# Layer 0's context gate and up in scaled fp16 parts, with their weights scanned in the projection's weight ring

## Chip, cores and metric

The kernel runs on one core of one Trainium2 chip. The metric is the device time in microseconds (us) of one execution; the median of the runs counts, and lower is better. The engines are TensorE (PE, matmuls), VectorE (DVE), ScalarE (ACT), GpSimd (POOL) and SyncE (SP). SP, ACT and POOL each issue DMAs from a queue of their own; an engine runs its rows in the order in which they stand.

## The reference

Two layers of a diffusion backbone over 1024 latent tokens and 256 context tokens, width 1024, in float32. Layer 0 mixes the tokens (Fourier groups beside a Hyena convolution), layer 1 has a neighbourhood attention; each ends in a feed-forward layer:

```python
def mixer_ab(u, w_in, w_out, ...):
    p = u @ w_in
    y_f = fourier_mix(p[..., :FOURIER_CH])
    y_h = hyena_mix(p[..., FOURIER_CH:], ...)
    return jnp.concatenate([y_f, y_h], axis=-1) @ w_out

def swiglu(u, w_gate, w_up, w_down):
    return (jax.nn.silu(u @ w_gate) * (u @ w_up)) @ w_down
```

`w_in` has 16 blocks of 128 columns, `w_gate` and `w_up` have 22 each (D_FF is 2816). The change is in layer 0's `swiglu` for the 256 context tokens, and in what is done during `p = u @ w_in`.

## The kernel before

**Parts and pieces.** Activations lie with their channels on the 128 partitions, in 8 blocks of 128 channels (KB = 8), and in three pieces of columns: two of 512 latent tokens (0 and 1) and the 256 context tokens (2). Precision comes from two parts, high and low: a product takes three matmuls (high x high, high x low, low x high). Parts come in two sorts. `weights` (L372) loads a tile of 512 KB, casts it on ACT to fp32r (L352, the tile `wh`) and subtracts on DVE (L354, `wl`). `weights16` multiplies by a scale and makes two fp16 parts, on ACT (L1948) and DVE (L1949), in one tile `hl`; for this the largest sum of absolute values of the weights must be known beforehand.

**Rings.** The pool `pw` (L323) has four buffers with the tag "ws" (tiles as they are loaded), two of "wh" and two of "wl". A new tile of a tag waits until the tile that had its buffer has been read for the last time. Users of "ws" are the weights of the projection, the tiles of the condition's weights (`ada_w`), the matrices of the long convolution (`mat`, `cs`) and, from the feed-forward layer on, `weights16`. `ld` (L333) issues on SP, `lda` (L336) on ACT, `ldr` (L339) on POOL.

**Order of the work.** A scheduler orders the instructions of each engine from the program's order and its own model of times; `follow(ins)` (L288) asks it to put instructions behind another one. The program's order is that of `run` (L2785):

- `in_proj` (L1104) goes through the 16 blocks of `w_in`: the first two as a pair, then one by one (loop over i, the text's block i), 72 matmuls each (8 channel blocks x 3 products x 3 pieces). Between the channel blocks it steps through `fill`: generators of other work (long filters, context filters, the condition's groups) with a number of steps for each i. From block 4 on a block ends in `short_conv` (L1087; ACT L1097, then DVE): its result z is spilled by SP, three DMAs for each z.
- Then the rest of the fill is drained; `turned` (L1306) transposes inputs, and `unit` (L1345) makes the long convolution with matmuls (L348) against matrices that `cast` loads through POOL and that `cmat2` (L416) casts on ACT.
- The output projection follows (`out_proj`, L1749). After each of its pieces it calls `after1`, which norms that piece for the feed-forward layer.
- `ffn(0)` (L2141) begins with the context stage: for each of 22 blocks a tile of gate and one of up, 24 matmuls of 256 columns each, Silu (L2188) and product. On the way each weight tile's absolute values are summed on ACT (L381, Abs with an accumulated sum, its output thrown away). After the 22 blocks `scale_w` (L1941 and around) makes the scales from these sums, by a reduction over the partitions on POOL and a chain on DVE. The latent tokens' part of gate and up needs the scales: it runs in scaled fp16 parts (L2095).
- Then down (its context part is L2484), the attention, and the second layer's feed-forward part, whose weights are scanned by `scan` (L1877) during `ffn(0)`: loads on ACT's queue into two tiles of another pool, one Abs each.

Of the kernel before, what the change touches and what calls it, by code (L numbers as in the profile page):

```python
# [13 lines left out]
AF = mybir.ActivationFunctionType  # L14
ALU = mybir.AluOpType
AX = mybir.AxisListType.X
MUL, ADD, SUB, MAX, MIN = ALU.mult, ALU.add, ALU.subtract, ALU.max, ALU.min

P = 128
D = 1024  # L20
KB = D // P
LAT = 1024
CTX = 256
NFB = 22
# [234 lines left out]
class Builder:  # L259
# [1608 lines left out]
    def scan(self, tiles, mark):  # L1868
# [4 lines left out]
        for k in range(n + 2):  # L1873
# [5 lines left out]
                    self.lda(t, tiles[k][0])  # L1879
            yield  # L1880

    def scale_u_begin(self):

        nc = self.nc
        t = self.cw[:, 20:28]
        for c in (0, 1):
            for j in (0, 1):
                nc.vector.tensor_reduce(t[:, 2 * j + c:2 * j + c + 1], self.ada[(1, c)][:, j * 8:j * 8 + 8], axis=AX, op=MAX,
                                        apply_absolute_value=True)
        nc.gpsimd.partition_all_reduce(t[:, 4:8], t[:, 0:4], channels=P, reduce_op=bass.bass_isa.ReduceOp.max)  # L1890
        return t
# [33 lines left out]
        self.turn = not getattr(self, "turn", False)  # L1925
        return self.S2() if self.turn else x()

    def scale_w(self, key, groups):

        nc = self.nc  # L1930
        sums = self.wsc[key]
        n = sums.shape[1] // 2
        nc.gpsimd.partition_all_reduce(sums[:, n:], sums[:, :n], channels=P, reduce_op=bass.bass_isa.ReduceOp.max)
        for j, k in enumerate(groups):
            t = self.C(2)
            s, inv = t[:, 0:1], t[:, 1:2]
            w = n // len(groups)
            nc.vector.tensor_reduce(s, sums[:, n + j * w:n + j * w + w], axis=AX, op=MAX)
            nc.vector.tensor_scalar(s, s, 1e-30, 1.0 / 8192.0, op0=MAX, op1=MUL)
            nc.vector.tensor_tensor(inv, s, self.xinv, MUL)  # L1940
            nc.vector.reciprocal(s, s)  # L1941
            self.wsc[k] = s, inv

    def split_scaled(self, src, t, s):

# [195 lines left out]
    def ffn(self, l, u, h, hs, second, after, keep=None, begun={}):  # L2141
# [29 lines left out]
        if u is None:  # L2171
            mx = self.mx
        else:
            wsums = self.C(4 * NFB)
            self.mx = mx = wsums[:, :8 * n2 - 4]
        if l == 0:
            self.pad(self.pt, PAD_T)
        if u is not None:
            self.wsc["here"] = wsums
            for fb in range(NFB):  # L2180
                wide = 3 if fb < NFB - 2 else 2
                gh, gl = self.weights(a["gate"][l, fb], wide=wide, sums=wsums[:, fb:fb + 1])
                uh, ul = self.weights(a["up"][l, fb], wide=wide, sums=wsums[:, NFB + fb:NFB + fb + 1])
                lo = self.last_lo
                ga = self.lin(gh, gl, 0, range(KB), u, (2,))[2]
                ua = self.lin(uh, ul, 0, range(KB), u, (2,))[2]
                t = self.T()
                nc.scalar.activation(t[:, :256], ga[:, :256], AF.Silu)  # L2188
                nc.vector.tensor_tensor(t[:, :256], ua[:, :256], t[:, :256], MUL)
                self.ldr(hidc[fb // 2][:, fb % 2], t[:, :256])  # L2190
                if fb >= 2:
                    with self.follow(last):
                        next(second, None)
                last = lo
            self.scale_w("here", [(0, 0), (0, 1)])
            self.load_cond(act=False)
            todo = self.ada_stream([(l1, m, (0, 1) if l1 == 0 or m < 2 else (0,))
                                    for l1, m in [(0, 5)] + [(1, m) for m in range(6)]], 30)
# [586 lines left out]
    def run(self):  # L2785
# [10 lines left out]
        def drain(g):  # L2796
            for _ in g:
                pass
# [21 lines left out]
        def filters():  # L2820
            gens = [self.filter_raw("l", raws["l"], (o,)) for o in (0, 1)]
            next(gens[0])
            yield
            for o in (0, 1):
                tot = self.filter_sum("l", o, raws["l"][o])
                for k, _ in enumerate(gens[o]):
                    if k > 1 and k % 2 == 0:
                        next(tot)
                    yield
                for k, _ in enumerate(self.spectrum_l(o, raws["l"][o], tot)):  # L2830
                    if o == 0 and k == 5:
                        next(gens[1])
                    yield

        long = filters()
        ada = self.late_groups((2, 3), "ws")
        filt = (x for o in (0, 1) for g in (self.filter_raw("c", raws["c"], (o,)), self.spectrum_c(o, raws["c"][o]))
# [8 lines left out]
        def conv():  # L2846
# [5 lines left out]

        fc, cc = four(), conv()
        self.in_proj(u, ng, ((long, (1, 2, 4, 5, 5, 5, 5, 5, 6, 0)), (filt, (0,) * 9 + (3, 3, 3, 3, 2)),
                             (ada, (0,) * 5 + (1, 1, 2, 1, 2, 1, 2, 1, 2, 1, 2))), fc, cc)
        self.held = False
        for i in range(8):
            self.tap(f"u{i}", u.ap(0, i, 0))
# [46 lines left out]
        uf = Act()  # L2905
# [10 lines left out]
        def after1(pcs):  # L2916
            spill(h, hs0, pcs)
            if 2 in pcs:
                uf.t.update(self.new_act(pcs=(2,)).t)
                rs = self.rms(pcs)  # L2920
                for b in range(KB):
                    self.norm_block({b: h.ap(0, b, 2)}, b, 2, 0, 3, uf, rs[0])
                self.half.add(0)
                self.scale_x(0, 3)
                load_h((1,))
                rest.append(rs[1])
            else:
                drain(first)
                rest.append(self.rms((1,))[0])
# [257 lines left out]
```

## Time and profile before

| | us |
|---|---|
| median of 3 runs (lowest, highest) | 2808.63 (2808.47, 2810.5) |
| profiled execution | 2803.95 |
| its span in the trace | 2802.2 |
| PE busy | 2692.3 |
| DVE busy | 2128.0 |
| ACT busy | 1629.4 |
| POOL busy | 507.4 |

The granted clock of the profiled execution is 0.986 of full speed. In the lines of the trace, the first number is the start in us from the span's start, the second a duration; then come the engine, the line of the kernel, the operation, output <- input, partitions x elements and type, and xN for N such instructions in a row. In brackets stands the engine's idle time before, and what ended it. In the window rows each engine has its busy us and, in brackets, its instructions. In the group rows stand, after the bar, the total busy us and the mean ns of one, then the idle time before. Matmuls overlap, so the price of one is read from the distance between starts.

### The profile page before, as it was taken

How to read it: one execution, taken by the hardware profiler on the slowest of the kernel's cores; microseconds unless marked ns; L12 is line 12 of the kernel's file. 1: busy time of each engine (PE TensorE's matmuls, PEld its weight loads, DVE VectorE, ACT ScalarE, POOL GpSimd, SP SyncE). 2: the span in 40 equal slices, each digit the busy share in tenths (PEclk: the TensorE clock that was granted, in tenths of full speed). 3: DMA queues.
4: the chain of work that ended last, by engine and by line, in shares of the span. 5: the costliest groups of instructions: out<-in, count | busy, mean ns of one | idle time of the engine just before them, and what ended most of it. 6: DMA issues, size and time to landing. Idle time of an engine off the chain costs nothing. (4 is left out here: it accounts for less than half of the span.)

```text
span 2802.2 us, 44493 instructions
## 1 busy us (share of the span) xinstructions
PE 2692.3 (96%) x15570; PEld 1713.0 (61%) x15570; DVE 2128.0 (76%) x3870; ACT 1629.4 (58%) x3005; POOL 507.4 (18%) x805
## 2 busy tenths in 40 slices
PE   7999789999999999999999999999999999999998
PEld 3877577878899444444446646767677544444444
DVE  6678788768877889986898736878786877775774
ACT  4434224443488566666656736888774656664653
POOL 0210233351101111121011002333221012221000
PEclk9999899999999999999999999999999999999999
DMA  7345636766645787787987746788955246654863
GB/s 273 111 156 171 190 106 186 231 205 224 232 162 172 257 297 288 284 313 268 362 311 278 237 155 160 190 207 196 252 180 196 85 144 223 222 193 167 296 223 105
DMA packets 312318, 595.92 MB, mean 213 GB/s; under 512 B 83353, under 2 KB 130139, under 8 KB 312095
## 3 DMA queue, kind: packets, MB, share of 16 engines
q1 hardware_dynamic: 242238, 381.76, 42.7%
q0 software_dynamic: 51456, 149.99, 15.4%
q10 hardware_dynamic: 18400, 61.35, 6.2%
q8 instruction: 122, 2.00, 0.3%
q14 instruction: 102, 0.83, 0.1%
HBM read 445.64 MB, written 119.80 MB: 202 GB/s over the span
## 5 line engine op out<-in xcount | busy, mean ns | idle before, releaser
L2095 PE MATMUL ps<-s,s 128*128 128x512 f16 x2280 | 509.0, 379 | 6.3 <-DVE s L2119 3.6
L2095 PEld LDWEIGHTS <-s 128*128 128x128 f16 x2640 | 258.1, 98 | 321.2 <-issue 11.1
L348 PE MATMUL ps<-s,wh 128*128 128x256 f32 (+1 forms) x1784 | 409.8, 333 | 7.9 <-ACT wh L352 5.8
L348 PEld LDWEIGHTS ps<-s,wh 128*128 128x128 f32 x1784 | 298.9, 191 | 43.1 <-ACT wh L352 8.4
L2359 PE MATMUL ps<-s 128*128 128x512 f16 (+2 forms) x1404 | 316.1, 376 | 0.2 <-ACT s L2349 0.2
L2359 PEld LDWEIGHTS <-s 128*128 128x128 f16 x1716 | 166.2, 98 | 196.1 <-issue 5.3
L348 PE MATMUL ps<-s,wl 128*128 128x256 f32 (+1 forms) x892 | 272.6, 332 | 3.5 <-DVE wl L354 3.5
L2349 ACT ACTIVATE s<-s,c 128x512 f16<-128x512 f32 (+1 forms) x300 | 200.3, 715 | 116.9 <-DMA s<-d 63.0
L348 PE MATMUL ps<-s,s 128*128 128x65 f16 (+4 forms) x2748 | 241.6, 239 | 17.2 <-DVE s L2722 3.8
L2350 DVE SCALAR_TENSOR_TENSOR s<-s,c,s 128x512 f16<-128x512 f32 (+1 forms) x300 | 208.7, 749 | 30.6 <-ACT s L2349 30.3
L339 POOL DMA_DIRECT2D d<-s x245 | 132.9, 544 | 503.9 <-DVE s L2212 169.7
L2095 PE MATMUL ps<-s,hl 128*128 128x512 f16 x924 | 212.2, 379 | 1.7 <-ACT hl L1948 1.7
L348 PE MATMUL pq<-s,hl 128*128 128x512 f16 (+1 forms) x960 | 208.0, 360 | 0.4 <-DVE s L2602 0.4
L348 PEld LDWEIGHTS ps<-s,wl 128*128 128x128 f32 x892 | 167.6, 191 | 22.4 <-DVE wl L354 5.2
L2095 PEld LDWEIGHTS <-hl 128*128 128x128 f16 x1056 | 103.2, 98 | 126.4 <-ACT hl L1948 1.9
L1948 ACT ACTIVATE hl<-ws,c 128x1024 f16<-128x1024 f32 x89 | 101.8, 1144 | 109.6 <-DMA ws<-in_up 39.1
L1949 DVE SCALAR_TENSOR_TENSOR hl<-ws,c,hl 128x1024 f16<-128x1024 f32 x89 | 114.0, 1284 | 62.3 <-ACT hl L1948 62.1
L348 PEld LDWEIGHTS <-s 128*128 128x128 f16 x2400 | 115.1, 98 | 66.0 <-issue 4.6
L348 PEld LDWEIGHTS ps<-s,s 128*128 128x128 f32 (+1 forms) x828 | 128.8, 192 | 33.8 <-PE ps L348 8.9
L1949 DVE SCALAR_TENSOR_TENSOR s<-t,c,s 128x512 f16<-128x512 f32 x176 | 127.0, 750 | 26.4 <-ACT s L1948 26.4
L348 PEld LDWEIGHTS <-hl 128*128 128x128 f16 x960 | 87.0, 98 | 81.0 <-issue 10.0
L1948 ACT ACTIVATE s<-t,c 128x512 f16<-128x512 f32 x176 | 118.1, 714 | 9.2 <-DVE t L2074 5.6
(538 smaller groups left out, 5109.4 us busy)
## 6 DMA issues: line engine op xcount, KB each, us to landing
s<-d SPq DMA_DIRECT2D x326, 256.0 KB, 4.8
d<-s POOLq DMA_DIRECT2D x229, 256.0 KB, 4.4
s<-in_down SPq DMA_DIRECT2D x150, 256.0 KB, 5.9
ws<-in_gate SPq DMA_DIRECT2D x42, 512.0 KB, 4.7
ws<-in_up SPq DMA_DIRECT2D x42, 512.0 KB, 6.3
s<-in_ada_w POOLq DMA_DIRECT2D x34, 512.0 KB, 6.5
d<-s SPq DMA_DIRECT2D x60, 256.0 KB, 2.8
s<-in_ada_w ACTq DMA_DIRECT2D x30, 512.0 KB, 7.7
```

The costliest lines, as they stand in the source:

```text
L339: self.last_ldr = self.nc.gpsimd.dma_start(out, in_).ins
L348: self.last_mm = self.nc.tensor.matmul(o, l, r, start=st, stop=sp).ins
L1948: self.last_hi = self.nc.scalar.activation(hi, src, AF.Copy, scale=s).ins
L1949: self.last_lo = self.nc.vector.scalar_tensor_tensor(lo, src, s, hi, op0=MUL, op1=SUB).ins
L2095: nc.tensor.matmul(ps, x[:, sl], y, start=first and j == 0 and x is wh and y is xh, stop=j == 3 and x is wl, skip_group_check=True)
L2349: self.last_hi = nc.scalar.activation(x, f[:, c:c + 512], AF.Copy, scale=s).ins
L2350: self.last_lo = nc.vector.scalar_tensor_tensor(y, f[:, c:c + 512], s, self.raw_part(x), op0=MUL, op1=SUB).ins
L2359: m = nc.tensor.matmul(acc[j][:, c0:c1], x[:, sl], y[:, xs], start=first and k == 0, stop=last and k == 2, skip_group_check=True)
```

## The change

Two things are changed together.

First, the context stage takes its gate and up tiles through `weights16` in place of `weights`: two scaled fp16 parts in `hl`, from the ring "ws". The context's activations `uf` become fp16 parts too. The scales are thus needed before the stage: `after1` calls `scale_both` (scales for the activations of latent and context tokens together) and `scale_w`, which stood after the 22 blocks; `scale_x` goes. Silu takes the inverse scale of gate, and the product with up that of up. The number of matmuls stays.

Second, the sums of absolute values come from a pass of their own over the 44 tiles, `scan_ring`: it loads each tile on ACT's queue into the ring "ws" and sums it with an Abs on ACT, two loads ahead. It is one more generator of the fill of `in_proj`, with 6 steps in each of the positions 2 to 5 of the fill (24 steps, which run during the blocks 3 to 6); the rest is drained right after `in_proj`, and POOL's reduction over the partitions follows there.

```diff
+    def scan_ring(self, tiles, mark):
+        nc = self.nc
+        n = len(tiles)
+        st = []
+        for k in range(n + 2):
+            with self.follow(mark()):
+                if k > 1:
+                    t = st.pop(0)
+                    nc.scalar.activation(t, t, AF.Abs, accum_out=tiles[k - 2][1])
+                if k < n:
+                    st.append(self.W("ws", "ws"))
+                    self.lda(st[-1], tiles[k][0])
+            yield
...
+    def scale_both(self, m):
...
+        nc.gpsimd.partition_all_reduce(r, t, channels=P, reduce_op=bass.bass_isa.ReduceOp.max)
...
+        for c in (1, 0):
+            ad = self.ada[(0, c)][:, m * 8:m * 8 + 16]
+            nc.vector.tensor_scalar(ad, ad, s[:, c:c + 1], None, op0=MUL)
+        self.xinv, self.xinv_c = x[:, 0:1], x[:, 1:2]
...
@@ ffn @@
-            self.wsc["here"] = wsums
+            (sg, _, cg), (su, _, cu) = self.wsc[(0, 0)], self.wsc[(0, 1)]
             for fb in range(NFB):
-                wide = 3 if fb < NFB - 2 else 2
-                gh, gl = self.weights(a["gate"][l, fb], wide=wide, sums=wsums[:, fb:fb + 1])
-                uh, ul = self.weights(a["up"][l, fb], wide=wide, sums=wsums[:, NFB + fb:NFB + fb + 1])
+                gh, gl = self.weights16(a["gate"][l, fb], sg)
+                uh, ul = self.weights16(a["up"][l, fb], su)
...
-                nc.scalar.activation(t[:, :256], ga[:, :256], AF.Silu)
-                nc.vector.tensor_tensor(t[:, :256], ua[:, :256], t[:, :256], MUL)
+                nc.scalar.activation(t[:, :256], ga[:, :256], AF.Silu, scale=cg)
+                nc.vector.scalar_tensor_tensor(t[:, :256], ua[:, :256], cu, t[:, :256], op0=MUL, op1=MUL)
...
-            self.scale_w("here", [(0, 0), (0, 1)])
@@ run @@
+        sums = self.wsc["here"] = self.C(4 * NFB)
+        scan = self.scan_ring([(a[x][0, fb], sums[:, j * NFB + fb:j * NFB + fb + 1]) for j, x in enumerate(("gate", "up"))
+                          for fb in range(NFB)], lambda: self.last_hi)
...
-                             (ada, (0,) * 5 + (1, 1, 2, 1, 2, 1, 2, 1, 2, 1, 2))), fc, cc)
+                             (ada, (0,) * 5 + (1, 1, 2, 1, 2, 1, 2, 1, 2, 1, 2)), (scan, (0, 0, 6, 6, 6, 6, 0))), fc, cc)
+        drain(scan)
+        self.scale_w_begin("here")
...
@@ after1 @@
-                uf.t.update(self.new_act(pcs=(2,)).t)
+                for b in range(0, KB, 2):
+                    uf.t.update(self.new_act16(2, b).t)
+                self.scale_both(3)
                 rs = self.rms(pcs)
+                self.scale_w("here", [(0, 0), (0, 1)], True)
...
-                self.scale_x(0, 3)
```

What the scheduler makes of it, at three places. The first is SP's queue. Here it is before, early in the projection: the rows `ws_...<-in_w_in` load the weights of the blocks 2, 3, 4, 5 and then 6; `d_...<-s2_...` are spills of the first two blocks.

```order
L333 DMA ws_233_765<-in_w_in 128x1024
L333 DMA ws_296_1037<-in_w_in 128x1024
L333 DMA ws_351_1270<-in_w_in 128x1024
L333 DMA ws_425_1562<-in_w_in 128x1024
L333 DMA d_104_334<-s2_162_496 128x256
L333 DMA d_106_335<-s2_163_499 128x256
L333 DMA s2_209_733<-in_cgf_l 128x128
L333 DMA ws_515_1884<-in_w_in 128x1024
L333 DMA ws_561_2073<-in_ada_w 128x1024
```

And SP's queue in the changed kernel, at the place where the weights of block 5 stand (`ws_439_1597`); the rows `d_114_339<-...` are the three spills of block 4's z.

```order
L333 DMA s2_404_1441<-in_skiprow 1x512
L333 DMA d_413_1460<-s2_415_1461 128x512
L333 DMA d_416_1464<-s2_418_1465 128x512
L333 DMA d_114_339<-s2_425_1526 128x256
L333 DMA ws_439_1597<-in_w_in 128x1024
L333 DMA d_114_339<-s2_426_1530 128x512
L333 DMA d_114_339<-s2_427_1534 128x512
```

Block 5's weights moved from the first group of loads to behind the first spill of block 4's z; in the same way block 6's now stand behind the spills of block 5's z, and block 7's behind those of block 6's.

The second place is ACT around block 4's z, in the changed kernel: L1097 makes z, L1891 is the scan's Abs, L336 a load of the scan, L352 casts of the fill. Block 5's weights `ws_439_1597` take the buffer of `ws_421_1493`; the fourth tile of that ring is `ws_422_1496`.

```order
L1097 ACTIVATE s2_425_1526<-ps_362_1293,c_102_332 128x256
L336 DMA ws_422_1496<-in_gate 128x1024
L1891 ACTIVATE ws_419_1469,c_100_331<-ws_419_1469 128x1024
L1097 ACTIVATE s2_426_1530<-ps_363_1294,c_104_334 128x512
L1097 ACTIVATE s2_427_1534<-ps_364_1295,c_104_334 128x512
L352 CAST s2_428_1540<-ps_430_1542 128x256
L352 CAST s2_428_1540<-ps_431_1551 128x256
L1891 ACTIVATE ws_420_1481,c_100_331<-ws_420_1481 128x1024
L336 DMA ws_423_1508<-in_gate 128x1024
L1891 ACTIVATE ws_421_1493,c_100_331<-ws_421_1493 128x1024
L352 CAST s2_432_1560<-pq_434_1562 128x256
L352 CAST s2_432_1560<-pq_435_1571 128x256
```

Before, the same three rows of z are followed by the casts of the fill alone. On PE, twelve matmuls of the fill moved from behind block 5's first matmul to ahead of it. Two tiles of the scan that are loaded in block 6 get their Abs only in the drain, so two of the ring's four buffers are left to the blocks 7 to 15.

The third place is ACT between the projection's last z (L1097) and the casts of the long convolution's matrices (L416). Before:

```order
L1097 ACTIVATE s2_1077_4124<-pq_1039_3959,c_100_331 128x256
L1097 ACTIVATE s2_1078_4128<-ps_1040_3960,c_102_333 128x512
L1097 ACTIVATE s2_1079_4132<-ps_1041_3961,c_102_333 128x512
L352 CAST s2_1082_4144<-t_1081_4142 128x512
L416 CAST mat_1181_4446<-cs_1180_4444 128x1024
L416 CAST mat_1182_4448<-cs_1180_4444 128x1024
```

And now, the end of the drain:

```order
L1891 ACTIVATE ws_1144_4312,c_100_331<-ws_1144_4312 128x1024
L336 DMA ws_1148_4324<-in_up 128x1024
L1891 ACTIVATE ws_1145_4315,c_100_331<-ws_1145_4315 128x1024
L336 DMA ws_1149_4327<-in_up 128x1024
L1891 ACTIVATE ws_1146_4318,c_100_331<-ws_1146_4318 128x1024
L336 DMA ws_1150_4330<-in_up 128x1024
L1891 ACTIVATE ws_1147_4321,c_100_331<-ws_1147_4321 128x1024
L1891 ACTIVATE ws_1148_4324,c_100_331<-ws_1148_4324 128x1024
L1891 ACTIVATE ws_1149_4327,c_100_331<-ws_1149_4327 128x1024
L1891 ACTIVATE ws_1150_4330,c_100_331<-ws_1150_4330 128x1024
L416 CAST mat_1227_4580<-cs_1226_4578 128x1024
L416 CAST mat_1228_4582<-cs_1226_4578 128x1024
```

All 22 Abs of the drain, with 20 loads between them and the casts of `turned`, now stand between the last z and the first L416. The matrix of the first unit matmul, which POOL loads, takes the buffer of `ws_1147_4321`, the 17th of the 20 tiles; the tile `cs_1226_4578` takes that of `ws_1149_4327`.

More of the change, by code (lines that the diff above doesn't have):

```diff
@@ L1926, in either, with scale_w_begin, scale_w @@
         return self.S2() if self.turn else x()
-    def scale_w(self, key, groups):
+    def scale_both(self, m):
+        nc = self.nc
+        t, r, s = self.cw[:, 32:36], self.cw[:, 36:40], self.cw[:, 40:42]
+        for c in (0, 1):
+            for j in (0, 1):
+                nc.vector.tensor_reduce(t[:, 2 * j + c:2 * j + c + 1],
+                                        self.ada[(0, c)][:, (m + j) * 8:(m + j) * 8 + 8], axis=AX, op=MAX,
+                                        apply_absolute_value=True)
+        nc.gpsimd.partition_all_reduce(r, t, channels=P, reduce_op=bass.bass_isa.ReduceOp.max)
+        x = self.cw[:, 44:46]
+        nc.vector.scalar_tensor_tensor(x, r[:, 2:4], 32.0, r[:, 0:2], op0=MUL, op1=ADD)
+        nc.vector.tensor_scalar(x, x, 1e-30, 1.0 / 8192.0, op0=MAX, op1=MUL)
+        nc.vector.reciprocal(s, x)
+        for c in (1, 0):
+            ad = self.ada[(0, c)][:, m * 8:m * 8 + 16]
+            nc.vector.tensor_scalar(ad, ad, s[:, c:c + 1], None, op0=MUL)
+        self.xinv, self.xinv_c = x[:, 0:1], x[:, 1:2]
+    def scale_w_begin(self, key):
+        sums = self.wsc[key]
+        n = sums.shape[1] // 2
+        self.nc.gpsimd.partition_all_reduce(sums[:, n:], sums[:, :n], channels=P, reduce_op=bass.bass_isa.ReduceOp.max)
+    def scale_w(self, key, groups, both=False):
         nc = self.nc
@@ L1932, in scale_w @@
         n = sums.shape[1] // 2
-        nc.gpsimd.partition_all_reduce(sums[:, n:], sums[:, :n], channels=P, reduce_op=bass.bass_isa.ReduceOp.max)
+        if not both:
+            self.scale_w_begin(key)
         for j, k in enumerate(groups):
@@ L1940, in scale_w @@
             nc.vector.tensor_tensor(inv, s, self.xinv, MUL)
+            self.wsc[k] = s, inv
+            if both:
+                self.wsc[k] = s, inv, self.cw[:, 46 + j:47 + j]
+                nc.vector.tensor_tensor(self.wsc[k][2], s, self.xinv_c, MUL)
             nc.vector.reciprocal(s, s)
-            self.wsc[k] = s, inv
     def split_scaled(self, src, t, s):
@@ L2173, in ffn @@
         else:
-            wsums = self.C(4 * NFB)
+            wsums = self.wsc["here"]
             self.mx = mx = wsums[:, :8 * n2 - 4]
```

## Prediction

> **What bounds the kernel now.** I read the head of the page first, for the engine that fills the span.
>
> ```profile
> span 2802.2 us, 44493 instructions
> PE 2692.3 (96%) x15570; PEld 1713.0 (61%) x15570; DVE 2128.0 (76%) x3870; ACT 1629.4 (58%) x3005; POOL 507.4 (18%) x805
> ```
>
> TensorE (PE) is busy in 96% of the span, so whatever stops it counts nearly in full. That is an average, so I then cut the span by stages, with the windows view: the input projection with the filters (to 450), the step into the long convolution (443 to 465), the convolution and the output projection (465 to 770), and the feed-forward layer's context stage (about 770 to 902). The columns are the window, its length, then busy us and instructions of PE, PE's weight loads, DVE, ACT and POOL, the granted clock, the DMA share and GB/s.
>
> ```profile
> 90.00:150.00 60.00, 59.72 (x333) 51.79 (x334) 47.22 (x96) 27.92 (x58) 16.64 (x22) 1.00 0.44 143
> 220.00:450.00 230.00, 200.31 (x969) 160.57 (x968) 193.00 (x421) 78.81 (x146) 47.05 (x61) 0.95 0.51 157
> 443.00:465.00 22.00, 15.91 (x82) 12.93 (x81) 17.82 (x48) 14.16 (x29) 2.64 (x5) 0.78 0.84 255
> 465.00:770.00 305.00, 295.52 (x1569) 251.02 (x1569) 232.93 (x399) 141.09 (x211) 101.84 (x111) 0.99 0.64 218
> 780.00:800.00 20.00, 14.74 (x99) 13.77 (x99) 10.21 (x16) 18.10 (x33) 1.62 (x3) 0.83 0.59 191
> 800.00:820.00 20.00, 20.00 (x177) 20.00 (x177) 17.84 (x24) 17.83 (x30) 1.62 (x3) 0.99 0.50 165
> 840.00:890.00 50.00, 50.00 (x443) 50.00 (x442) 34.73 (x42) 44.64 (x75) 4.86 (x9) 1.00 0.57 185
> ```
>
> The context stage is bound by PE but for its start, where ACT is full (18.10 of 20) and PE is not. The projection's blocks between 90 and 150 have no spare PE time at all (59.72 of 60); after 220 PE stands idle for 29.7 us of 230, beside a DVE busy for 193. From 465 to 770 only 9.5 us of 305 are idle: a delay that arises before 465 is still there at 770.
>
> **Part 1: the context stage.** Gate and up take 1056 matmuls of 256 columns before and after; their operands become fp16. What a matmul costs is the distance between starts, not the duration shown. The first two rows are single steps of the stage as it is (three matmuls each), the other two bracket 124 fp16 matmuls of the same shape in the down projection's context part.
>
> ```profile
> 816.00 0.39 PE L348 MATMUL ps<-s,wh 128*128 128x256 f32 x2
> ...
> 816.34 0.39 PE L348 MATMUL ps<-s,wh 128*128 128x256 f32 x2
> ...
> 1521.80 13.70 PE L2484 MATMUL ps<-s,hl 128*128 128x256 f16 x124
> 1535.33 0.95 PE L348 MATMUL pq<-c,tk 128*128 128x1 f32 x8
> ```
>
> Now 0.34 / 3 = 113.3 ns; in fp16 13.53 / 124 = 109.1 ns. 1056 x 4.2 ns = 4.4 us gained. The start and the end of the stage, and the group of the Abs that the change takes out of it:
>
> ```profile
> 789.54 1.07 ACT L381 ACTIVATE t<-s 128x1024 bf16<-128x1024 f32 x1
> ...
> 793.20 1.04 ACT L352 CAST wh<-s 128x1024 fp32r<-128x1024 f32 x1
> ```
>
> ```profile
> 794.29 0.80 PE L348 MATMUL ps<-s,wh 128*128 128x256 f32 x2 [4.80 <-ACT wh L352]
> ...
> 795.93 0.63 PE L348 MATMUL ps<-s,wh 128*128 128x256 f32 x2
> ...
> 796.58 0.63 PE L348 MATMUL ps<-s,wh 128*128 128x256 f32 x2
> ...
> 800.34 0.41 PE L348 MATMUL ps<-s,wh 128*128 128x256 f32 x2
> ```
>
> ```profile
> 901.91 1.15 ACT L1948 ACTIVATE hl<-ws,c 128x1024 f16<-128x1024 f32 x1 [3.04 <-DVE c L1941]
> ```
>
> ```profile
> 903.11 1.04 PE L2095 MATMUL ps<-s,hl 128*128 128x512 f16 x4 [1.73 <-ACT hl L1948]
> ```
>
> ```profile
> L381 ACT ACTIVATE t<-s 128x1024 bf16<-128x1024 f32 x44 | 46.0, 1048 | 0.0
> ```
>
> At the start PE waits 4.80 us for a weight cast that stands behind Abs (1.05 us each) and the casts of the activations on ACT, and then runs 24 matmuls from 794.29 to 800.34 where 24 x 113.3 ns = 2.7 us would do: 3.3 us lost, nearly all to a step of 0.65 in place of 0.34, in the window whose granted clock is 0.83. Without the Abs there I take all 8.1 us as gained (at worst 3: the casts of the activations stay). At the end PE waits 1.73 us for the chain of scale_w, which is now done long before: 1.7 gained. The added scale_both and scale_w in after1 stand where scale_x stood; they lie beside the output projection's matmuls, which hide them, and cost up to 3 if they do not. Part 1: -4.4 - 8.1 - 1.7 = -14 (from -8 to -15).
>
> **Part 2: the scan in blocks 3 to 6.** The scan's tiles take slots of the four-slot ring "ws" from which the projection's weights come, and a slot is free again only after its Abs on ACT. Loads of before on SP, the z activations and the condition's Silu on ACT, the first matmuls of blocks 5, 6 and 7 on PE, and the landing of such a load (the page's part 6); the last row serves for the step of a matmul of 512 columns:
>
> ```profile
> 32.77 7.73 SPq L333 DMA_DIRECT2D ws<-in_w_in  x4
> ...
> 91.51 0.33 SPq L333 DMA_DIRECT2D ws<-in_w_in  x1
> ...
> 131.52 0.33 SPq L333 DMA_DIRECT2D ws<-in_w_in  x1
> ```
>
> ```profile
> 160.89 1.92 ACT L1097 ACTIVATE s<-ps,c 128x256 f32<-128x256 f32 x3
> ...
> 202.08 1.93 ACT L1097 ACTIVATE s<-ps,c 128x256 f32<-128x256 f32 x3
> ...
> 225.97 1.89 ACT L1097 ACTIVATE s<-ps,c 128x256 f32<-128x256 f32 x3
> ...
> 229.45 2.20 ACT L553 ACTIVATE s<-s 128x512 f32<-128x512 f32 x4
> ```
>
> ```profile
> 162.65 0.47 PE L348 MATMUL ps<-s,wh 128*128 128x256 f32 x2 [0.26 <-DVE s L1099]
> ...
> 200.92 0.40 PE L348 MATMUL ps<-s,wh 128*128 128x256 f32 x2
> ...
> 224.25 0.50 PE L348 MATMUL ps<-s,wh 128*128 128x256 f32 x2
> ```
>
> ```profile
> ws<-in_w_in SPq DMA_DIRECT2D x16, 512.0 KB, 4.3
> ```
>
> ```profile
> 464.53 4.25 PE L348 MATMUL ps<-s,mat 128*128 128x512 f32 x15
> ```
>
> Before, the weights of blocks 5, 6 and 7 are issued at 32.77, 91.51 and 131.52, over 90 us ahead of use. In the new order each waits for an Abs that stands behind a z activation on ACT, and on SP behind that z's spill. Block 5: z4 is done at 160.89 + 1.92 = 162.8; three Abs (3.1) and two short casts (0.8) later the slot is free, 166.7; load 4.3, cast 1.04: PE could start at 172.0, not 162.65, +9.4. Twelve fill matmuls now stand ahead of it (12 x 4.25 / 15 = 3.4): +6. Block 6: z5 is done at 204.0; three Abs and two casts of 0.6 make 208.4, load and cast 213.7, against 200.92: +13. Block 7: its load stands behind the spills of z6 and needs the slot of a condition tile, which is worked on only after the Silu (229.45 + 2.20 = 231.6); load and cast give 237.0 against 224.25: +13. Early in the scan one Abs waits for its own load ahead of the casts of block 3's fill, with PE full: I put +3 (0 to 6.4, a whole landing). Together +35. The 29.7 us of idle PE after 220 take some back; DVE, which is what PE waits for there, has work of its own that the stalls do not stop, so I take half, 15: part 2 is +20 (5 to 35). Each new long stop of PE is followed by a slow stretch as at 794.29: 6.05 - 0.46 (a second wait there) - 2.7 = 2.9 us; for two stops (blocks 6 and 7) +6 (0 to 9). [...]
>
> **Part 3: the drain.** After the last block 22 Abs and 20 loads remain, ahead of the long convolution's first weights in the same ring.
>
> ```profile
> 447.12 1.46 ACT L1097 ACTIVATE s<-ps,c 128x512 f32<-128x512 f32 x2
> ...
> 460.20 4.00 ACT L352 CAST s<-ps 128x512 fp32r<-128x512 f32 x8
> ```
>
> ```profile
> s<-in_up ACTq DMA_DIRECT2D x22, 512.0 KB, 6.4
> ```
>
> ```profile
> GB/s 273 111 156 171 190 106 186 231 205 224 232 162 172 257 297 288 284 313 268 362 311 278 237 155 160 190 207 196 252 180 196 85 144 223 222 193 167 296 223 105
> ```
>
> The first unit matmul, at 464.53 now, needs a matrix in the slot of the drain's 17th load. ACT is free at 447.12 + 1.46 = 448.6; the two tiles held since block 6 go in 2.1, the first two loads land 6.4 later, 457, and are summed by 458. From there four slots turn in 6.4 + 1.05 us, 1.86 a tile: 15 tiles make 486, the matrix lands 4.3 later, 490: +25. A second way: 22 us x 255 GB/s = 5.6 MB move there already, 20 x 0.524 = 10.5 MB come on top; at the highest rate of a slice, 362 GB/s, that is 44.5 us, +22. Were ACT alone the limit (22 x 1.05 + 4.0 from 448.6, then 4.3) it would be +15; at 255 GB/s, +41. I take +25, by the row for the landing. Behind the drain's Abs on ACT stand the casts of the next matrices (L416), for which the units wait as well, and on POOL the reduction over the partitions of the sums, for which nobody waits before the output projection. Little is idle after it (9.5 us of 305), so the delay stays.
>
> **Sum.** -14 + 20 + 6 + 25 = +37 on the profiled execution's 2803.95 is 2841; the median of the runs shown lies 4.7 above that execution: 2846.
>
> **Rivals.** (a) Faster: the ring never makes PE wait. ACT has the time (78.81 us busy of 230 after 220), so the Abs could run as tiles land and the convolution's start could be set by its turned inputs, as now. Then only part 1 counts: 2808.6 - 14 = 2795. It decides at block 5: if its load goes out ahead of z4. For it speaks ACT's idle share, against it that each queue runs its rows in the order listed. (b) The blocks absorb their late weights, since PE has fill work from the filters; the drain alone counts: 2808.6 - 14 + 25 = 2820. (c) The ring stays narrow: two of its slots are held by scan tiles from block 6 to the drain, so the blocks 7 to 15 have two for weights and condition tiles. If half of these nine wait for a load and a cast, 5.3 us each, +24 on the forecast: 2870. For it speaks that both kinds load on SP behind spills; against it, DVE's share there. (d) fp16 halves the matmul's price because the weight load sets it:
>
> ```profile
> L348 PEld LDWEIGHTS ps<-s,wh 128*128 128x128 f32 x1784 | 298.9, 191 | 43.1 <-ACT wh L352 8.4
> ...
> L2095 PEld LDWEIGHTS <-hl 128*128 128x128 f16 x1056 | 103.2, 98 | 126.4 <-ACT hl L1948 1.9
> ```
>
> At 113.3 x 98 / 191 = 58 ns the stage would win 58 us, not 4.4, and the sum would be 2846 - 54 = 2792. The row of 124 at 109.1 ns speaks against it. [...]
>
> **Chances and range.** Forecast 0.60, (a) 0.07, (b) 0.14, (c) 0.14, (d) 0.02, and 0.03 that stops and gain cancel to within 0.2% (5.6 us), about what a measurement of this kernel can tell from no change. Faster 0.09, same 0.03, slower 0.88. The low ends of the parts, -15 + 5 + 0 + 15, give +5: 2814; the high ends, -8 + 35 + 9 + 41, give +77: 2886. All ends together on one side are unlikely; 2815 to 2880 holds (b) and (c) and leaves out (a) and (d).
>
> **What would show it.** Right: between 160 and 240 three waits of PE for a weight cast (wh) that stands behind a late load of w_in; the first unit matmul at 505 to 520 (464.5 + 26 + 25), with some 20 Abs of about 1.05 us in front of it, four per landing; then the same distances as before up to the context stage; there a distance of 109 ns, no wait of 4.8 us at its start and none of 1.7 at its end. Wrong: the unit's first matmul within 10 us of 464.5, or the blocks 5 to 7 at their old times, would fell parts 3 or 2; a gain in the context stage beyond 20 us, or none, would fell part 1.

## Result and the profile after

The changed kernel takes 2873.09 us (median; 2871.46 to 2889.05), the kernel before 2809.57 us beside it: a ratio of 1.0236, with a 95% interval from 1.0215 to 1.0258. It is slower by 63.5 us; the forecast was 2846 us, slower by 37. Two single runs beside the experiments, one of the kernel before (3518.73 us) and one of `e11` (10361.11 us), were slow ones and are left out of the ratios. Below are the page's head, the same windows cut at the new times, and PE's waits in the projection and the drain (us in total, times, longest us).

```profile
span 2869.7 us, 44523 instructions
## 1 busy us (share of the span) xinstructions
PE 2694.6 (94%) x15570; PEld 1699.7 (59%) x15570; DVE 2135.9 (74%) x3875; ACT 1639.6 (57%) x3005; POOL 500.1 (17%) x805
```

```profile
90.00:150.00 60.00, 59.54 (x330) 51.31 (x329) 44.28 (x93) 30.87 (x64) 16.29 (x22) 1.00 0.48 165
150.00:220.00 70.00, 49.72 (x217) 36.46 (x215) 44.64 (x84) 32.45 (x62) 9.62 (x18) 0.87 0.65 216
220.00:480.00 260.00, 202.27 (x950) 163.63 (x949) 189.13 (x405) 84.97 (x157) 47.38 (x63) 0.89 0.52 160
480.00:560.00 80.00, 51.93 (x243) 41.28 (x242) 34.82 (x78) 43.51 (x81) 8.69 (x8) 0.78 0.73 263
560.00:840.00 280.00, 264.79 (x1425) 225.10 (x1424) 213.56 (x376) 128.86 (x194) 92.20 (x104) 0.98 0.60 202
```

```profile
PE ps L348 <- ACT wh L352: 38.5, 8, 11.8
PE ps L348 <- DMA mat<-in_vfo_l: 14.5, 1, 14.5
PE pq L348 <- ACT wh L352: 10.3, 1, 10.3
```

PE has as much work as before (2694.6 against 2692.3 us); the time is in waits. 48.8 us are nine waits for a weight cast `wh`, of which the kernel before has none in these stages: three at the blocks 5 to 7 (20.1 us) and six in the blocks 8 to 15 (28.7 us). One more wait, of 14.5 us, is for the first matrix of the long convolution. The blocks up to 150 are as full as they were. The waits start at block 5; here is its chain and that of the next two, on SP (loads), on ACT (casts) and on PE (first matmuls).

```profile
168.04 0.33 SPq L333 DMA_DIRECT2D ws<-in_w_in  x1
219.41 0.33 SPq L333 DMA_DIRECT2D ws<-in_w_in  x1
259.80 0.33 SPq L333 DMA_DIRECT2D ws<-in_w_in  x1
```

```profile
175.97 1.04 ACT L352 CAST wh<-ws 128x1024 fp32r<-128x1024 f32 x1 [4.89 <-DMA ws<-in_w_in]
...
225.86 1.04 ACT L352 CAST wh<-ws 128x1024 fp32r<-128x1024 f32 x1 [4.55 <-DMA ws<-in_w_in]
...
263.27 1.04 ACT L352 CAST wh<-ws 128x1024 fp32r<-128x1024 f32 x1 [4.89 <-DMA ws<-in_w_in]
```

```profile
170.62 4.56 PE L348 MATMUL pq<-s,tk 128*128 128x512 f32 x12 [7.35 <-ACT s L352]
...
177.07 2.27 PE L348 MATMUL ps<-s,wh 128*128 128x256 f32 x6 [1.89 <-ACT wh L352]
```

```profile
226.96 2.51 PE L348 MATMUL ps<-s,wh 128*128 128x256 f32 x6 [6.37 <-ACT wh L352]
```

```profile
264.37 2.50 PE L348 MATMUL ps<-s,wh 128*128 128x256 f32 x6 [11.81 <-ACT wh L352]
```

Each load goes out 3.5 to 8 us before its cast, where it went out 90 us and more before use; ACT stands idle for it (4.89, 4.55, 4.89), and the first matmul comes 1.1 us after the cast begins. Each of the three goes out at the moment at which its slot comes free: the last read of the tile before it, by an Abs (blocks 5 and 6) or by DVE's work on a condition tile (block 7), ends at 168.01, 219.39 and 259.76 us. In block 5 PE had waited 7.35 us before that for a cast of the fill, which stands behind Abs on ACT; the twelve matmuls that the scheduler moved ahead of the block are the row at 170.62.

The drain, on ACT (the first of its 22 Abs and the 19th, which frees the slot of the first matrix), on POOL (the load of the first matrix) and on PE, and the landing times of the drain's 20 loads:

```profile
501.81 1.07 ACT L1891 ACTIVATE ws<-ws 128x1024 f32<-128x1024 f32 x1
...
534.11 1.06 ACT L1891 ACTIVATE ws<-ws 128x1024 f32<-128x1024 f32 x1 [0.41 <-DMA ws<-in_up]
```

```profile
535.55 0.54 POOL L339 DMA_DIRECT2D mat<-in_vfo_l  x1 [59.38 <-DMA ws<-in_up]
```

```profile
539.74 5.46 PE L348 MATMUL ps<-s,mat 128*128 128x512 f32 x17 [14.49 <-DMA mat<-in_vfo_l]
```

```profile
DMA to landing us min/median/max: 3.8/5.3/6.3
```

And the window of the drain; its last two numbers are the busy share of the 16 DMA engines and GB/s:

```profile
505.00:540.00 35.00, 7.09 (x36) 5.44 (x35) 7.04 (x15) 28.64 (x58) 1.06 (x2) 0.60 1.02 385
```

The DMA engines have no idle time left in it (a share of 1.02, where 1 is all 16 of them busy).

The first unit matmul moved from 464.53 to 539.74. From the last z (L1097, 446.65 before, 499.51 now) it is 40.2 us, before 17.9: the drain costs 22.4. Last, PE at the start and the end of the context stage:

```profile
854.03 8.03 PE L348 MATMUL ps<-s,hl 128*128 128x256 f16 x72
...
965.75 5.40 PE L348 MATMUL ps<-s,hl 128*128 128x256 f16 x48
970.99 5.34 PE L2139 MATMUL ps<-s,hl 128*128 128x512 f16 x24
```

No bracket stands there any more: neither the wait of 4.8 us nor that of 1.7. The last 48 matmuls take 5.24 us, 109.2 ns each. The stage lasts 970.99 - 854.03 = 117.0 us; before it was 903.11 - 770.76 = 132.4.

So the traces' difference of 67.5 us splits into +52.9 in the projection (last z), +22.4 in the drain, +8.1 between the first unit matmul and the context stage (306.2 us before, 314.3 now) and -15.4 in the stage; after it 0.4 are left.

### The profile page after: what moved, and what is told of

Read it like the earlier page. It is cut to its first block, busy times and chain, and to the rows that moved or that the text cites. A ratio compares the mean times of both kernels' runs of the same rounds, so it can differ in the third digit from the quotient of the medians.

```text
span 2869.7 us, 44523 instructions
## 1 busy us (share of the span) xinstructions
PE 2694.6 (94%) x15570; PEld 1699.7 (59%) x15570; DVE 2135.9 (74%) x3875; ACT 1639.6 (57%) x3005; POOL 500.1 (17%) x805
## 5 line engine op out<-in xcount | busy, mean ns | idle before, releaser
L348 PE MATMUL ps<-s,wh 128*128 128x512 f32 (+1 forms) x1080 | 288.7, 376 | 39.7 <-ACT wh L352 39.7
L348 PEld LDWEIGHTS <-hl 128*128 128x128 f16 x2016 | 190.1, 98 | 93.8 <-issue 9.7
L348 PEld LDWEIGHTS ps<-s,wh 128*128 128x128 f32 x1080 | 193.1, 195 | 79.4 <-ACT wh L352 45.5
L1993 DVE SCALAR_TENSOR_TENSOR hl<-ws,c,hl 128x1024 f16<-128x1024 f32 x133 | 170.0, 1280 | 69.2 <-ACT hl L1992 68.3
L1992 ACT ACTIVATE hl<-ws,c 128x1024 f16<-128x1024 f32 x133 | 151.6, 1144 | 105.1 <-DMA ws<-in_up 36.6
L2139 PEld LDWEIGHTS <-hl 128*128 128x128 f16 x1056 | 103.2, 98 | 124.6 <-issue 0.8
L348 PE MATMUL ps<-s,wl 128*128 128x256 f32 (+1 forms) x540 | 164.6, 366 | 3.1 <-DVE wl L354 3.1
L348 PEld LDWEIGHTS <-s 128*128 128x128 f16 x2400 | 114.2, 98 | 67.5 <-DMA s<-tk 6.4
L348 PE MATMUL ps<-s,hl 128*128 128x256 f16 x1056 | 115.8, 273 | 0.0
```

The costliest lines, as they stand in the source:

```text
L348: self.last_mm = self.nc.tensor.matmul(o, l, r, start=st, stop=sp).ins
L1992: self.last_hi = self.nc.scalar.activation(hi, src, AF.Copy, scale=s).ins
L1993: self.last_lo = self.nc.vector.scalar_tensor_tensor(lo, src, s, hi, op0=MUL, op1=SUB).ins
L2139: nc.tensor.matmul(ps, x[:, sl], y, start=first and j == 0 and x is wh and y is xh, stop=j == 3 and x is wl, skip_group_check=True)
```

## Experiments

Two theories stood against each other. The **ring theory**: what costs is the slots of "ws" which scan tiles hold while the weights of the blocks and the matrices of the convolution wait for them. The **work theory**: the 44 Abs on ACT (46 us) and their 23 MB of loads cost what they cost, wherever they are put. The table has, of each run, the median, the ratio to the kernel before with its interval, and from the trace the end of the last block's matmuls, the first unit matmul, the time from there to the context stage, and the length of the stage (us). The runs of the kernel before beside these lie between 2802 and 2817 us, with medians of 2808 to 2810. In the six traces in which no scan touches the blocks and nothing is late before them (before, `e2`, `e5`, `e6`, `e9`, `e11`) the last block ends at 445 to 453, and in all the traces of the table the program behind the context stage, which no run changes, takes 1896 to 1907 us: differences below some 8 us between single traces mean little.

| run | median | ratio (95%) | last block ends | first unit matmul | to the stage | stage |
|---|---|---|---|---|---|---|
| before | 2809.57 | | 444.8 | 464.5 | 306.2 | 132.4 |
| the change | 2873.09 | 1.0236 (1.0215-1.0258) | 499.9 | 539.7 | 314.3 | 117.0 |
| e1_two_passes | 2855.89 | 1.0158 (1.0134-1.0182) | 476.0 | 521.5 | 314.5 | 117.0 |
| e2_all_in_drain | 2864.39 | 1.0189 (1.0164-1.0214) | 447.5 | 530.1 | 313.9 | 117.0 |
| e3_no_scan | 2801.81 | 0.9969 (0.9957-0.9982) | 454.9 | 474.2 | 306.1 | 117.0 |
| e5_in_convolution | 2835.00 | 1.0085 (1.0069-1.0101) | 450.7 | 470.8 | 346.4 | 117.0 |
| e6_spread | 2837.90 | 1.0107 (1.0086-1.0127) | 453.1 | 475.2 | 342.9 | 117.0 |
| e7_weights_first | 2837.13 | 1.0096 (1.0074-1.0118) | 455.1 | 500.1 | 312.9 | 117.0 |
| e8_spread_in_blocks | 2811.52 | 1.0010 (0.9999-1.0021) | 458.5 | 483.0 | 308.4 | 117.0 |
| e9_no_scan_late | 2796.24 | 0.9957 (0.9942-0.9972) | 451.8 | 471.9 | 308.7 | 117.0 |
| e10_half_abs | 2871.45 | 1.0228 (1.0200-1.0255) | 499.2 | 539.2 | 317.2 | 117.0 |
| e11_before_no_abs | 2804.08 | 0.9981 (0.9966-0.9996) | 449.4 | 470.8 | 304.9 | 126.6 |
| e12_early_spread | 2815.03 | 1.0024 (1.0010-1.0037) | 469.4 | 487.2 | 308.9 | 117.0 |
| e14_spread_half_abs | 2805.39 | 0.9991 (0.9980-1.0002) | 454.1 | 472.0 | 307.9 | 117.0 |

**Two passes: no tile held from block 6 to the drain.**

```diff
-        scan = self.scan_ring([... for j, x in enumerate(("gate", "up"))
-                          for fb in range(NFB)], lambda: self.last_hi)
+        scan, rest_scan = [self.scan_ring([... for fb in range(NFB)],
+                                          lambda: self.last_hi) for j, x in enumerate(("gate", "up"))]
...
         drain(scan)
+        drain(rest_scan)
```

> The scan cut into two passes: the 22 gate tiles take the 24 steps of the blocks 3 to 6 and are finished there, the 22 up tiles go through the drain, so that no scan tile is held from block 6 to the drain. Ring theory (the cost is the held slots): the weights of blocks 8 to 15 come early again, the lateness of the last z falls from 53 us to 25 to 35, the drain costs its 22 to 25 as before: about 2848 us. Work theory (the cost is the Abs on ACT and the 23 MB of loads, wherever in the projection they stand): the same work, about 2873.

Measured 2855.9. PE's waits for `wh` fall from 48.8 us to this:

```profile
PE ps L348 <- ACT wh L352: 13.8, 3, 6.3
```

The blocks 5 and 6 begin about as late as in the change (+15.2 and +25.1 against before; in the change +14.4 and +26.0), block 7 begins 34.0 us late in place of 40.1, and from there the lateness no longer grows: the last block ends 31.2 late in place of 55.1, with no wait for `wh` behind block 7. The two held slots cost some 24 us, with the same Abs and loads. The drain, which now has two loads more, is 3.4 us longer (43.7 from the last z). The median lies between the two numbers expected, 8 above the ring theory's; the lateness of the last z, 31.2, is the ring theory's (25 to 35).

**Nothing in the blocks, all 44 tiles in the drain.**

```diff
-(scan, (0, 0, 6, 6, 6, 6, 0))
+(scan, (0,))
```

> No scan step during the blocks, all 44 tiles in the drain. Ring theory: the blocks have their old times (last z at 445 to 450 us), the drain turns 44 tiles at the 1.6 to 1.9 us a tile of now, so the first unit matmul comes at 520 to 535, +55 to +70; with the 15 us that the context stage gains about 2850 to 2865. Work theory: the same Abs and loads cost the same as spread out: 2873, with the last z late as well or the drain longer by as much.

Measured 2864.4. The blocks are back at their old times (block 5 at 163.0, 6 at 200.9, 7 at 224.2), and the drain alone brings the first unit matmul to 530.1, +65.6, with one wait:

```profile
PE ps L348 <- DMA mat<-in_vfo_l: 53.4, 1, 53.4
```

Without scan tiles in the ring the blocks are not late. The total lies at the upper end of the ring theory's 2850 to 2865 and only 8.7 below the change: 44 tiles in a drain are themselves expensive, and this run alone hardly separates the theories.

**Weights asked for one block earlier** (on top of the two passes).

```diff
+        with self.follow(self.ada_ld):
+            nxt = self.weights(a["w_in"][order[2]])
         for i, nb in enumerate(order[2:], 2):
-            with self.follow(self.ada_ld):
-                wh, wl = self.weights(a["w_in"][nb])
+            wh, wl = nxt
+            if i < 15:
+                with self.follow(self.ada_ld):
+                    nxt = self.weights(a["w_in"][order[i + 1]])
```

> The two passes again (gate in the blocks 3 to 6, up in the drain), and each block's weights are asked for one block earlier in the program, ahead of the scan steps of the block before. Same Abs, same loads. Late-load theory (what is left of the lateness, 31 us, is the weights of the blocks 5 to 7 that wait for a slot): no wait of PE for a weight cast of more than 3 us in these blocks, last z at 445 to 455 us, total 2856 - 25 = 2831 (2825 to 2838). Work theory: unchanged, about 2856.

Measured 2837.1, 18.8 less than the two passes. The blocks 5, 6 and 7 begin 3.9, 5.4 and 7.7 us late, the total is within the late-load theory's range, and of the waits for `wh` this is left (the 2.7 us are at block 8):

```profile
PE ps L348 <- ACT wh L352: 3.2, 2, 2.7
```

The load that waits for a slot was the cause of the late blocks 5 to 7: the same Abs and loads remain, only the order in which the ring is asked has changed.

**The drain: ACT's rows or the loads?**

```diff
-                    t = st.pop(0)
+                    t = st.pop(0)[:, :1024 if k < 24 else 512]
```

> The changed kernel, but the drain's Abs read 512 of the 1024 columns (left out: half of these sums); the loads are the same. If ACT's rows set the pace of the drain, 22 x 0.5 = 11 us go: 2862. If the landing of the loads sets it (four slots in 6.4 + 1.05 us, the prediction's working), 2 to 3 us go: 2870.

Measured 2871.5 (the change: 2873.1). The last z on ACT and the first unit matmul on PE:

```profile
498.80 0.56 ACT L1097 ACTIVATE s<-pq,c 128x256 f32<-128x256 f32 x1 [0.64 <-PE pq L348]
```

```profile
539.18 6.06 PE L348 MATMUL ps<-s,mat 128*128 128x512 f32 x14 [20.90 <-DMA mat<-in_vfo_l]
```

40.4 us, as long as with whole Abs (40.2). ACT is free for 0.43 us of each Abs, and nothing is won, not even the 2 to 3 us that the turning of the slots was expected to give: the loads set the pace, and not ACT's rows. The window of this drain is as full of DMA work as the one of the change:

```profile
505.00:540.00 35.00, 6.45 (x30) 5.34 (x29) 6.49 (x12) 20.00 (x55) 1.06 (x2) 0.58 1.00 381
```

With slots that come free sooner the loads land later (median 5.7 us in place of 5.3) at the same rate, 381 against 385 GB/s. So the busy DMA engines, and not the number of slots, look like the limit; a drain with more slots was not run.

**No scan at all.** Two runs; the sums are a constant.

```diff
-        scan = self.scan_ring(...)
+        nc.gpsimd.memset(sums[:, :2 * NFB], 30.0)
+        scan = iter(())
```

> No scan at all: the sums are set to a constant (left out: the pass over the weights, so the scales are not those of the data). Both theories: the projection and the step to the first unit matmul have their old times, the context stage takes 117 us in place of 132: 2794 (2792 to 2797). If the 8 us that the convolution lost after the drain belong to the fp16 parts and not to the drain, 2802.

The median is 2801.8, above what was expected, though the stage takes its 117.0. In the trace block 5 begins 11.0 us late, and the reason stands at the program's start: POOL's reduction, whose input is now there at once, starts at 18.43 us, and DVE's reading of it (L1979) stands in DVE's rows ahead of the filters' network, which waits behind it. The sine chain of that network (ACT L784) is 11 us later than in the kernel before, which the last row shows.

```profile
18.43 0.52 POOL L1966 PARTITION_ALL_REDUCE c<-c  x1 [8.85 <-issue]
```

```profile
18.98 0.26 DVE L1979 TENSOR_REDUCE c<-c 128x1 f32<-128x22 f32 x2 [17.99 <-POOL c L1966]
```

```profile
24.69 0.74 ACT L784 ACTIVATE s<-s 128x640 f32<-128x640 f32 x1 [20.55 <-DMA s<-in_ada_k]
```

```profile
13.53 0.74 ACT L784 ACTIVATE s<-s 128x640 f32<-128x640 f32 x1 [9.46 <-DVE s L782]
```

So the constant was made from a tile of the convolution instead:

```diff
+        nc.vector.tensor_scalar(sums[:, :2 * NFB], self.tr[0][0][:, :2 * NFB].bitcast(F32), 0.0, 30.0, op0=MUL, op1=ADD)
+        self.scale_w_begin("here")
         units = [self.unit(1, fb, cls, ...
```

> Once more without the scan (left out: the pass over the weights; the sums are a constant), but the constant is made from a tile of the long convolution, so that POOL's reduction stands there and not at the program's start, where it cost the first such run some 10 us. Both theories: 2809 less the 15.4 us of the context stage, 2794 (2790 to 2799), first unit matmul at 463 to 467, 306 us from there to the context stage.

2796.2, as expected, though the first unit matmul came at 471.9 and not at 463 to 467. L784 is back at 13.3 us. But by the end of the context stage the two traces without a scan are level (897.3 and 897.5 us), so that the 5.6 us between their medians come from the program's start is not shown. The first half of the change by itself wins 13.1 us in the medians, 15.4 in the stage. All that makes the change slower is the scan: 2873.1 - 2796.2 = 76.9 us.

**The context stage before, without its Abs.**

```diff
-                gh, gl = self.weights(a["gate"][l, fb], wide=wide, sums=wsums[:, fb:fb + 1])
+                gh, gl = self.weights(a["gate"][l, fb], wide=wide)
...
+            nc.vector.tensor_scalar(wsums[:, :2 * NFB], u.ap(0, 0, 2)[:, :2 * NFB].bitcast(F32), 0.0, 30.0, op0=MUL, op1=ADD)
```

> The kernel before, without the sums of absolute values in its context stage (left out: the 44 Abs; the sums are a constant made from the stage's activations); the matmuls stay in fp32r. Theory of the prediction (of the stage's gain 4.4 us are the matmuls, the rest is Abs and the scales' chain): the wait of 4.8 us at the start and the slow stretch go, the stage takes 121 to 125 us in place of 132.4, total 2799 to 2803. Rival (the fp16 parts themselves or the activations' casts bring it): 130 to 133, 2808.

Measured 2804.1, and the stage 126.6: 5.8 us less, just outside what the theory gave. The waits that remain on PE:

```profile
795.85 0.50 PE L348 MATMUL ps<-s,wh 128*128 128x256 f32 x2 [1.40 <-ACT wh L352]
...
797.37 0.38 PE L348 MATMUL ps<-s,wl 128*128 128x256 f32 x1 [1.02 <-DVE wl L354]
```

The wait of 4.80 shrinks to 1.40 but does not go: the weight cast still stands behind casts of the activations on ACT. The rest of the stage's gain, 9.6, comes with the fp16 parts: 4.3 by the matmuls' distance, 2.4 by these two waits, and the remaining 2.9 was not taken apart.

**The scan elsewhere: in the convolution.** Two tiles of another pool; three steps behind each unit of the first order and two behind each of the second, or one at each yield of a unit.

```diff
-        scan = self.scan_ring(... lambda: self.last_hi)
+        scan = self.scan(... lambda: self.last_mm)
...
             for _ in self.unit(0, fb, cls):
                 pass
+            for _ in range(3):
+                next(scan)
```

> The whole scan moved out of the projection and the drain: 44 tiles through two tiles of another pool, three steps after each unit of the first order, two after each of the second, the rest in the last inverse, marked by the last matmul. Ring theory: ACT (141 us busy of 305 there) and the queues have room, the ring is not touched: 2794 to 2802, faster than before. Work theory: 46 us of Abs and 23 MB cost a good part of what they cost now: above 2820.

> As the run with the scan in the convolution, but one step at each yield of a unit in place of three in a row behind it. Head-of-line theory (ACT runs its rows in order, and an Abs that stands one or two rows behind its own load holds up the casts behind it: 42 us of ACT idle for these loads in that run): the loads have 6 us or more before their Abs, the convolution loses 0 to 15 us in place of 40, total 2797 to 2812. Work theory (46 us of Abs and 23 MB have to be paid there): unchanged, 2830 to 2838.

Measured 2835.0 and 2837.9; the ring theory's 2794 to 2802 fails, and so does the mend by spreading; both times lie where the work theory had them (above 2820; 2830 to 2838). What ACT waited for ahead of these Abs (us, times), with the steps in a row:

```profile
  DMA s<-in_up: 23.2, 15
  DMA s<-in_gate: 18.7, 9
```

and with the steps spread, where the longest wait of PE behind it is for a cast of the spectrum (L1302):

```profile
  DMA s<-in_up: 23.8, 12
  DMA s<-in_gate: 21.1, 13
```

```profile
PE ps L1453 <- ACT s L1302: 12.0, 1, 12.0
```

In both, ACT stands 42 to 45 us before an Abs whose load has not landed, and what stands behind it on ACT starts after it: in the run with the steps spread one such wait, 6.45 us, ends with the Abs at 553.75, and ACT's next rows start at 554.81 (a copy, L1408) and 555.28 (two casts, L416). Spreading the steps took nothing off these waits (41.9 us in 24 waits with the steps in a row, 44.9 in 25 with them spread), so these two runs do not separate the waiting from the 46 us of Abs.

**The scan spread over the blocks 3 to 15, weights early.**

```diff
-(scan, (0, 0, 6, 6, 6, 6, 0))
+(scan, (0, 0, 3, 3, 3, 4, 4, 4, 4, 4, 4, 4, 4, 4, 1, 0))
```

> Weights asked for one block earlier, and the 46 steps of the scan spread over the blocks 3 to 15, three or four a block; nothing of it is left for the drain. Ring theory: few waits of PE for weights, first unit matmul at 465 to 480, the context stage's 15 us are kept: 2794 to 2812. Work theory: the Abs and loads cost what they cost in two passes, 2831 or more.

Measured 2811.5, 61.6 less than the change and no difference to before that can be measured (1.0010, 0.9999 to 1.0021). Blocks 5, 6 and 7 begin 1.4, 1.8 and 4.9 us late, and there is no drain. In PE's list of waits the weights no longer stand first, but casts of the fill:

```profile
PE ps L348 <- ACT s L352: 12.0, 7, 3.0
PE ps L348 <- ACT g L352: 5.6, 1, 5.6
```

Against the run without a scan 15.3 us are left. Two more runs looked for them. The first puts the steps earlier and the reduction later:

```diff
+(scan, (0, 0, 5, 5, 5, 5, 5, 5, 5, 5, 5, 1, 0))
```

> Weights asked for one block earlier, the scan with five steps in each fill from the third to the eleventh, none in the last blocks, and the reduction after the first units. Ring theory: what the evenly spread run lost late (18 us at the first unit matmul) halves, 2798 to 2808; work theory: no change against it, 2811 or more.

2815.0, the work theory's number: not better, and the last block ends at 469.4. The second halves the Abs of the even spread:

```diff
-                    t = st.pop(0)
+                    t = st.pop(0)[:, :512]
```

> The evenly spread scan with early weights (2811.5 us, 15 above the run without a scan), its Abs cut to 512 of 1024 columns (left out: half of the sums); 44 x 0.5 = 22 us less of ACT's time, the same loads and ring. If what is left of the cost is ACT's time in front of the fill's casts, a half or more of the 15 us goes: 2800 to 2805. If it is the loads (the Abs that wait for them, the ring, the traffic), it stays: 2809 to 2814.

2805.4, 6.1 less than with whole Abs, at the edge of the first range expected: ACT's time in front of the fill's casts carries some 6 of the 15 us, and what the other 9 are stays open. No version with a whole scan beat the kernel before. Of the 77 us that the scan costs, 61 thus go with the order in which the ring is asked and with the drain, as the ring theory has it; for the other 15, and for the scan in the convolution, the work theory is not refuted.

## Why the prediction was right in direction and short in size

**Part 1, the context stage (-14): right.** Measured -15.4. The matmuls' distance of 109.1 ns, read from another stage of the kernel before, came out at 109.2, and both waits went. That 8.1 us stand on Abs alone was too much: without Abs the stage wins 5.8.

**Part 2, late weights in the blocks 5 to 7 (+35, and +6 for the slow clock): right in sum within 1 us, by smaller errors that cancel, which is luck.** Block 7 began 40.1 us late. Block 5's share was larger than worked out (14.4 against 3 + 6): its load went out at 168.04, near the 166.7 of the working, but its cast began only 7.9 us later and not 4.3, with scan loads beside it, and a cast of the fill held PE for 7.35 before. The blocks 6 and 7 added 11.6 and 14.1, against 16 each with the slow clock. The granted clock was 0.50 in the first 3 us of both (226.96 to 229.96 and 264.37 to 267.37), as it was from 794.29 to 797.29 before; the first six matmuls of each take 2.30 us, six such at 234.79 take 1.17. The third of the waits ends at 264 and not by 240, since the delays add up. The slots that come free just before the three loads, and the runs with two passes and with early weights, show the mechanism.

**Part 2, after block 7: the sum lacked the held slots.** With 15 us taken back, the forecast had the end of the last block 26 us late; it was 55.1 late. Here is the stretch from the first matmul of block 7 to that end, before, in the change and with two passes:

```profile
224.25:444.79 220.54, 193.62 (x931) 155.18 (x931) 186.80 (x409) 73.60 (x139) 46.18 (x60) 0.95 0.48 150
264.37:499.94 235.57, 196.67 (x935) 159.25 (x935) 183.31 (x403) 67.51 (x129) 45.26 (x59) 0.91 0.46 138
258.24:475.97 217.73, 197.31 (x926) 159.23 (x927) 179.79 (x390) 66.07 (x126) 45.77 (x59) 0.92 0.48 147
```

PE is idle for 26.9, 38.9 and 20.4 us of it (the length less PE's busy time). In the change 28.7 us of that are the six new waits for weights, so the old waits fell to 10.2 us: the 15 us that the prediction took back did come back (16.7). What its sum put at nothing is the mechanism of the rival (c), given 0.14: two slots held by scan tiles starve the blocks 8 to 15. The working gave (c) +24; the six waits are 28.7, and without the held slots the last block ends some 24 us earlier, of which 6 us show at block 7 already. The remaining 3.0 are slower matmuls, at a granted clock of 0.91 in place of 0.95, a term within the scatter of single traces: 40.1 + 28.7 - 16.7 + 3.0 = 55.1.

The idle time was still no safe reserve. With no slot held (the third row), only 6.5 of the 26.9 us came back, and 3.7 of these went into slower matmuls. In the other six traces with no scan in the blocks PE is idle for 23.2 to 26.5 us of this stretch. Nor is DVE what PE mostly waits for there: of the 26.9 us before, 17.2 end with work on ACT, its casts above all, and 9.5 with DVE. Why more came back in the change is only argued: while PE stands for weights, the fill's casts get ahead of it.

**Part 3, the drain (+25): right in size.** Measured +22.4. `e10` shows that it is not ACT's rows. Whether it is four slots, as in the first way of the working, or the rate of the loads, as in the second, is not told apart by a run; the DMA engines without idle time speak for the second.

**"So the delay stays" after the drain: short by 8.1 us in the change.** Every run with a drain needs 313 to 317 us from the first unit matmul to the context stage, every run without one and with the convolution left alone 305 to 309. In the change's trace 5.7 of the 8.1 us are more idle time of PE (15.2 us against 9.5). What in the convolution is slower behind a drain was not tried.

**The sum.** The two spans differ by 67.5, 30.5 more than forecast: 29.1 at the end of the last block, less 2.3 up to the last z, -2.6 in the drain, +8.1 behind it, -1.4 in the stage and -0.4 after it. (c)'s 2870 is 3 us from the result; its mechanism happened, but the 8.1 us were in no sum, so a part of that closeness is luck.

**Rivals.** (a) did not happen in any run with a whole scan; in the change SP issued block 5's load where it is listed, at 168.04, behind the first spill of z4 (the third of three issues from 161.91) and ahead of the other two (168.46). (b), the blocks absorbing late weights, did not happen: the last block ends 55.1 us late in the change and 31.2 with two passes, and early weights (`e7`) take most of that away. (d) is refuted by the 109.2 ns: weight loads in fp16 took 98 ns in the stage against 191 before, and the distance of the matmuls moved by 4 ns.

## What to carry to other kernels

A ring of tiles that was sized for one stream is not free memory for a second: a load that used to go out 90 us ahead of use goes out when the guest's tile is released, and the guest's last tiles can hold slots through the whole stage (some 24 us here). Ask for the tiles on the critical path ahead of the guest's, leave no tile of the guest waiting in the ring while it stands still, and do not leave a rest of its pass as a drain in front of the next stage; early weights and an even spread without a drain brought back 61 of 77 us. And do not book idle time of the bound engine later in a stage as a reserve for a delay earlier in it, unless the trace shows what that idle time waits for.

## What the runs showed of the hardware that was not expected

Halving 22 Abs of 1.06 us in a row of loads changed the time from the last z to the first unit matmul by 0.2 us (40.2 and 40.4), with the DMA engines at a busy share of 1.02 and 1.00 and 385 and 381 GB/s. In `e3` a reduction over the partitions on POOL at 18.43 us, 8.85 us after POOL's instruction before it, delayed a chain of DVE and ACT (L775 to L784) by 11 us that uses nothing of it: DVE's reading of the reduction stood ahead of the chain and waited 17.99 us. In the run in which the reduction stands later, L784 starts at 13.3 us, as before. Why POOL's reduction itself started no earlier was not tried.
